# Modulation columns of the first layer: from VectorE accumulation to one-column TensorE products in three of five groups

## The chip, the cores and the metric

The kernel runs on one core of a Trainium2 chip. The metric is the device time of one execution in microseconds, the median of three runs. A profiled execution is one further run, traced by the hardware profiler. The engines are TensorE (PE, with its weight loads as PEld), VectorE (DVE), ScalarE (ACT), GpSimd (POOL) and SyncE (SP), whose queue issues the DMAs.

## The reference

The model is a trunk of two layers over 1024 tokens of width 1024, float32. At the head of each layer stands a modulated norm (adaLN), which is all that the change concerns:

```python
c_act = jax.nn.silu(c)                       # (1, 1024)
mod = c_act @ w_ada + b_ada                  # (1, 3072)
shift, scale, gate = jnp.split(mod[:, None, :], 3, axis=-1)
h = rms_norm(x, norm_g) * (1.0 + scale) + shift
proj = h @ w_in
```

The projection feeds three token mixers (pooling, retention, RWKV-7), each with a SiLU gate path; their outputs are projected, merged by sigmoid gates, projected once more, scaled by `gate` and added to x. A final RMSNorm closes the trunk.

`mod` is a product of one vector with a 1024 x 3072 matrix: very few operations on 12 MB of weights per layer.

## The kernel before

**Layout.** Features lie on the 128 partitions, tokens on the free axis. x is held as 8 tiles (kt 0 to 7, 128 features each) by 2 halves of 512 tokens. Each large product is done in three passes (high x high, low x high, high x low parts in fp32r) by `mm1` and `mm3`, and every TensorE product goes through `mmul` (line 394 of the profile).

**Modulation.** The 24 columns of `mod` (128 features each) are cut into seven groups, the list `ADA`: group 0 is scale columns 8 and 9, group 1 scale columns 10 and 11, group 2 scale columns 12 to 15, group 3 shift columns 0 to 3 (tiles kt 0 to 3), group 4 shift columns 4 to 7 (tiles kt 4 to 7), groups 5 and 6 the gate. The generator `ada` makes one group: for each kt one VectorE operation (line 216 for the first, line 218 for the other seven) multiplies a 128 x (n*128) slice of the weights by one column of the activated c and adds it to an accumulator `ada_acc`; then n TensorE products against a column of ones sum over the partitions into `adaps`, and VectorE adds the bias (line 226), and for scale columns also forms `acoef` (line 231). Each `next` on the generator does one kt, the last one the end.

**The head of layer 0, written out by hand.** From `with tc.manual_schedule` on, TensorE, VectorE, ScalarE and GpSimd work in the order in which the code stands. The norm is postponed: the first three projection tiles (low-rank, k and r of head pair 0) are computed from x scaled by `acoef` alone (`scaled`, lines 1146 and 1147; `mms(h, kt)`, blocks of nine products of 512 columns for one tile kt of half h). Meanwhile the squares of x are summed (`sq`, line 1124 on GpSimd); `rstd_task` sums them over the partitions on TensorE (`ssps`, four one-column products), takes the root on ScalarE (line 538) and the reciprocal on VectorE (line 539), and spreads the result over the partitions by four TensorE products (`rbc`). `rstd_copy` copies it to `rbs` (ScalarE, line 1157). `first_raw` multiplies the three projections by it (line 1167), and `normed` multiplies x by it (line 1176): half 0 wholly on GpSimd, half 1 four tiles on VectorE and four on GpSimd. `shifted(h, kt)` applies scale and shift and splits the result in high and low parts (lines 1184 to 1189); it needs the shift columns, group 3 for kt 0 to 3 and group 4 for kt 4 to 7. With these parts the next two projection tiles are made (`mm1` for the first of them, tile by tile for half 0). `shift_bias` makes the part of the first three projections that comes from the shift (lines 1205 and 1207).

The steps of groups 0 to 4 (`gs[0]` to `gs[4]`) are set between these. SyncE's queue loads their weights in the same order: groups 0 to 2 and two tiles of group 3 through a ring of eight slots (`ringG`), six tiles of group 3 into buffers that later hold weights (`wada`), group 4 again through the ring, then the six raw weight tiles for `shift_bias`. A ring load waits until the slot's last user has read it.

**Behind the head.** A planner orders the projection tiles and the mixers' tasks, from modelled costs and due times; a tile scheduler places the instructions. Groups 5 and 6 and all groups of layer 1 are made by `ada` on VectorE as before, in a lane of their own.

Of the kernel before, what the change touches and what calls it, by code (L numbers as in the profile page):

```python
# [17 lines left out]
P = 128  # L18
# [4 lines left out]
HF = 512  # L23
NKT = D // P
# [56 lines left out]
ADA = []  # L81
# [8 lines left out]
def trunk_kernel(ctx, tc, xT, cvec, pos, vecs, consts, w_ada, w_all, pool_w, lora_w, out):  # L90
# [16 lines left out]
    def nm(s):  # L107
        uid[0] += 1
        return f"{s}_{uid[0]}"

    def slot(tag, n, w=HF):
        def f(s, dt=F32):
            return tp.tile([P, w], dt, tag=tag, name=nm(s), bufs=n)

        return f

    t_rk = slot("rk", 4)
    t_lt = slot("lt", 4)
# [3 lines left out]
    t_vp = slot("vp", 2)  # L122
# [4 lines left out]
    def mx(s):  # L127
        t = ps_m.tile([P, HF], F32, tag="mx", name=nm(s))
        if len(mxq) == 2:
            behind[t.name] = mxq.popleft()  # L130
        mxq.append(t.name)
        return t
# [10 lines left out]
    cact = cp.tile([P, 8], F32, name="cact")  # L143
    nc.sync.dma_start(out=cact, in_=cvec)
    o = CST["bone"]
# [52 lines left out]
    def ada_load(l, g, slot_, ws, n):  # L198
        for _ in range(n):
            w = slot_("wada")  # L200
            nc.sync.dma_start(out=w, in_=w_ada[l, ADA[g][2] + len(ws)])
            ws.append(w)

    def ada(l, g, slot_, gap=2200, acc_=t_lt, ws=None):
        c, n, _ = ADA[g]
        W_ = n * P
        acc = acc_("ada_acc")[:, 0:W_]
        late = ws is None
        ws = [] if late else ws
        for kt in range(NKT):  # L210
            i, o = divmod(kt * W_, HF)
            if late and o == 0:
                ada_load(l, g, slot_, ws, min(i + 2, 2 * n) - len(ws))
            w = ws[i][:, o : o + W_]
            if kt == 0:
                nc.vector.tensor_scalar_mul(acc, w, cact[:, 0:1])
            else:
                nc.vector.scalar_tensor_tensor(acc, w, cact[:, kt : kt + 1], acc, op0=ALU.mult, op1=ALU.add)  # L218
            yield gap
        if late:  # L220
            yield wait(acc)
        ps = mx("adaps")
        for m in range(n):
            mmul(ps[:, m : m + 1], acc[:, m * P : (m + 1) * P], ones)
        o = VEC["b_ada"]
        nc.vector.tensor_tensor(mod[l][:, c : c + n], ps[:, 0:n], vec[l][:, o + c : o + c + n], op=ALU.add)
        if c >= 16:
            nc.vector.tensor_scalar_mul(mod[l][:, c : c + n], mod[l][:, c : c + n], 0.5)
        if 8 <= c < 16:
            o = VEC["norm_g"] + c - 8  # L230
            nc.vector.scalar_tensor_tensor(
                acoef[l][:, c - 8 : c - 8 + n], mod[l][:, c : c + n], 1.0, vec[l][:, o : o + n],
                op0=ALU.add, op1=ALU.mult,
            )
        yield

    def run(gen):
        for _ in gen:
            pass
# [117 lines left out]
    def wait(*aps):  # L357
        settle()
        names = [x.tensor.name if hasattr(x, "tensor") else x.name for x in aps]
        if len(mxq) == 2:  # L360
            names.append(mxq[0])
        return max(0.0, max(ready.get(n, 0.0) for n in names) - clock[0])
# [24 lines left out]
    def mmul(out, lhsT, rhs, start=True, stop=True, **kw):  # L387
        n = rhs.free_size()
        fast = rhs.dtype == F32R
        settle()  # L390
        await_(out, lhsT, rhs)
        m = lhsT.free_size()
        clock[0] += (n + 32) / 2.4 if fast else 2 * max(n, 1.6 * m - 92, m - 16) * 0.875
        nc.tensor.matmul(out, lhsT=lhsT, rhs=rhs, start=start, stop=stop, **kw)  # L394
# [113 lines left out]
    def acc_ps():  # L508
        return ps_a.tile([P, HF], F32, tag="acc", name=nm("acc"))
# [579 lines left out]
    def evac(*a):  # L1089
        run(evac_steps(*a))  # L1090
# [59 lines left out]
    def mms(h, *kts):  # L1150
        for kt in kts:
            for i in range(3):
                mm1(acc6[h][i], wparts[i][kt // 4], kt % 4, h_cur[h][kt], kt == 0, kt == 7)
# [74 lines left out]
    with tc.manual_schedule(engines={ET.PE, ET.DVE, ET.Activation, ET.Pool}):  # L1228
        acc6.append([acc_ps() for _ in range(3)])
        acc6.append([ps_c.tile([P, HF], F32, tag=t, name=nm("acc"), bufs=n) for t, n in (("cy", 2), ("cy", 2), ("ch", 1))])  # L1230
        aw = [[] for _ in range(5)]
        gs = [ada(0, g, None, acc_=t_vp if g == 4 else t_lt, ws=aw[g]) for g in range(5)]

        def aload(g, n):
            ada_load(0, g, wada_slot, aw[g], n)

        aload(0, 4)
        nc.sync.dma_start(out=vec[0], in_=vecs[0])
        wdma(0, 0)
        wsp(0, 0)  # L1240
        xdma(0, 0, 1)
        wdma(0, 1, 2)
        xdma(1, 0, 1)
        aload(1, 4)
        xdma(0, 2, 3)
        xdma(1, 2, 3)
        steps(gs[0], 9)
        derive(0)
        scaled(0, 0)
        wsp(0, 1)  # L1250
        steps(gs[1], 3)
        scaled(0, 1)
        wsp(0, 2)
        steps(gs[1], 5)
        mms(0, 0, 1)
        sq(0, 0)
        sq(0, 1)
        steps(gs[1], 1)
        scaled(1, 0, 1)
        sq(1, 0)  # L1260
        sq(1, 1)
        mms(1, 0, 1)
        aload(2, 8)
        for h in range(2):
            for kt in (2, 3):
                steps(gs[2], 2)
                scaled(h, kt)
                sq(h, kt)
        mms(0, 2, 3)
        wdma(1, 0, 1, 2)  # L1270
        xdma(0, 4, 5, 6, 7)
        nc.sync.dma_start(out=cst, in_=consts[:, 0 : CST["bone"]])
        xdma(1, 4, 5, 6, 7)
        wsp(1, 0, 1, 2)
        mms(1, 2)
        steps(gs[2], 1)
        mms(1, 3)
        for tag in ("wh", "wl"):
            for _ in range(3):
                w = wp.tile([P, HF], F32, tag=tag, name=nm("wada"), bufs=3)  # L1280
                ada_load(0, 3, lambda _: w, aw[3], 1)
        aload(3, 2)
        for kt in range(4, 8):
            sq(0, kt)
            scaled(0, kt)
            mms(0, kt)
        for kt in range(4, 8):
            sq(1, kt)
            scaled(1, kt)
            steps(gs[3], 2)  # L1290
        wprep(True)
        aload(4, 8)
        r0 = rstd_task([ssum[0]], rbc[0])
        r1 = rstd_task([ssum[1]], rbc[1])
        mms(1, 4)
        next(r0)
        mms(1, 5)
        run(r0)
        rstd_copy(0)
        steps(gs[3], 1)  # L1300
        steps(gs[4], 2)
        for i in range(3):
            first_raw(0, i)
            steps(gs[4], 1)
        normed(nc.gpsimd, 0, 0, 1, 2, 3, 4, 5, 6, 7)
        mms(1, 6)
        next(r1)
        steps(gs[4], 1)
        shifted(0, 0)
        steps(gs[4], 1)  # L1310
        shifted(0, 1)
        steps(gs[4], 1)
        mms(1, 7)
        run(r1)
        shifted(0, 2, 3)
        rstd_copy(1)
        sb = shift_bias()
        next(sb)
        first = [wready.popleft()]
        wprep()  # L1320
        first.append(wready.popleft())
        pss = {}
        for i in range(2):
            pss[i, 0] = acc_ps()
        for kt in range(4):
            mm1(pss[0, 0], first[0][1][kt // 4], kt % 4, h_cur[0][kt], kt == 0, kt == 7)
        steps(gs[4], 1)
        for kt in range(4, 8):
            shifted(0, kt)
            mm1(pss[0, 0], first[0][1][kt // 4], kt % 4, h_cur[0][kt], kt == 0, kt == 7)  # L1330
        normed(nc.vector, 1, 0, 1, 2, 3)
        normed(nc.gpsimd, 1, 4, 5, 6, 7)
        for j in range(2):
            mm3(pss[1, 0], first[1][1][j], h_cur[0][4 * j : 4 * j + 4], j == 0, j == 1)
        pss[0, 1] = acc_ps()
        for kt in range(8):
            shifted(1, kt)
            mm1(pss[0, 1], first[0][1][kt // 4], kt % 4, h_cur[1][kt], kt == 0, kt == 7)
        L_ = (0, {}, {}, [])
        evac(first[0][0], pss[0, 0], 0)  # L1340
        pss[1, 1] = acc_ps()
        for j in range(2):
            mm3(pss[1, 1], first[1][1][j], h_cur[1][4 * j : 4 * j + 4], j == 0, j == 1)
# [17 lines left out]
    for l in range(L):  # L1361
# [26 lines left out]
        while wready[0][0] != ("merge",):  # L1388
            it, ws = wready.popleft()
# [65 lines left out]
        while wready[0][0][0] != "out":  # L1455
            it, ws = wready.popleft()
# [5 lines left out]
            elif it[0] == "gate":  # L1462
                n, d = it[1], it[2]
                for h, ps in enumerate(in_tile2(ws)):
                    nc.scalar.activation(gate_tile((n, d, h)), ps, AF.Tanh, scale=0.5)
            else:
                n, d0 = it[1], it[2]
# [5 lines left out]
                for d, h in dh:  # L1473
                    ps = acc_ps()
                    mm3(ps, ws[d - d0], [osplit[n][k][h] for k in range(4)], True, True)
                    o = (d % 2) * T + h * HF
                    m = mt[d // 2][:, o : o + HF]
# [26 lines left out]
        for part, (h, sl) in enumerate(parts):  # L1504
# [3 lines left out]
            for i, d in enumerate(out_order(l, part)):  # L1508
                it, ws = wready.popleft()
# [15 lines left out]
                ps = acc_ps()[:, 0 : xr.free_size()]  # L1525
# [129 lines left out]
```

## Time and profile before

| | us |
|---|---|
| median of 3 runs (lowest, highest) | 2536.18 (2535.82, 2540.87) |
| profiled execution | 2538.03 |
| its span | 2536.3 |
| PE busy, share of the span | 2417.6, 95% |
| DVE busy | 1394.0, 55% |
| ACT busy | 796.6, 31% |
| POOL busy | 847.6, 33% |
| mean granted TensorE clock | 0.971 |

How to read it: the busy time of TensorE includes time at a lower clock. The granted clock is 1.00 at full speed and 0.50 when the throttle halves it. In the timeline a row gives start, duration, engine, line, operation, output and inputs, shape, count, and in brackets how long the engine was idle before and what ended that. Rows that follow each other on TensorE overlap, because products are pipelined: the price of one is the distance from start to start.

### The profile page before, as it was taken

Reading aid. Unit: us, or ns where it says so; the run is one execution under the profiler, and the core shown is the slowest. Engines: PE = TensorE matmul, PEld = TensorE weight load, DVE = VectorE, ACT = ScalarE, POOL = GpSimd, SP = SyncE. Lnnn points to the kernel's source line nnn. Section 1 sums busy time; section 2 is a strip of 40 time slices with the busy share of each in tenths; the row PEclk is TensorE's granted clock in tenths of the full one; section 3 lists DMA queues with packets and bytes.
Section 4 is the critical chain, followed back from the end, with each engine's and each line's share of the span. In section 5 each row is a group of like instructions: output and inputs, shape, how many; then the busy total and the mean of one; then the engine's idle time right before and its main releaser. Section 6 shows DMA issues by size and latency. Waiting matters only on the chain. (4 is left out here: it accounts for less than half of the span.)

```text
span 2536.3 us, 34936 instructions
## 1 busy us (share of the span) xinstructions
PE 2417.6 (95%) x13318; PEld 1995.5 (79%) x13318; DVE 1394.0 (55%) x2588; ACT 796.6 (31%) x1482; POOL 847.6 (33%) x729
## 2 busy tenths in 40 slices
PE   6889999999899999999999999999999999999998
PEld 4677887787788788877878787788878778787888
DVE  7886358357547935267455735844744663412344
ACT  4642232233224222212353223223322322221243
POOL 5522223133133332364452222322313322236441
PEclk9799999999999999999999999999999989999999
DMA  6222112011112413666541211211211121354342
GB/s 229 76 88 71 38 38 84 28 40 64 55 35 83 133 47 130 189 212 195 170 126 34 80 34 38 68 41 35 86 45 38 60 79 51 117 158 122 105 152 76
DMA packets 125080, 225.25 MB, mean 89 GB/s; under 512 B 14192, under 2 KB 17520, under 8 KB 124912
## 3 DMA queue, kind: packets, MB, share of 16 engines
q1 hardware_dynamic: 124912, 223.01, 27.8%
q8 instruction: 105, 1.72, 0.3%
q14 instruction: 63, 0.52, 0.1%
HBM read 176.03 MB, written 46.92 MB: 88 GB/s over the span
## 5 line engine op out<-in xcount | busy, mean ns | idle before, releaser
L513 POOL TENSOR_TENSOR wl<-wr,wh 128x512 fp32r<-128x512 f32 x338 | 450.3, 1333 | 1220.2 <-ACT wh L512 1123.0
L394 PE MATMUL acc<-hhi,wh 128*128 128x512 f32 x1968 | 799.5, 406 | 29.1 <-DVE k L981 29.1
L394 PE MATMUL acc<-hlo,wh 128*128 128x512 f32 x1968 | 801.7, 407 | 0.0
L394 PE MATMUL acc<-hhi,wl 128*128 128x512 f32 x1968 | 799.2, 406 | 0.0
L394 PEld LDWEIGHTS acc<-hhi,wh 128*128 128x128 f32 x1968 | 377.7, 192 | 100.4 <-DVE k L981 31.6
L512 ACT CAST wh<-wr 128x512 fp32r<-128x512 f32 x338 | 209.3, 619 | 734.3 <-PE acc L394 476.0
L394 PEld LDWEIGHTS acc<-hhi,wl 128*128 128x128 f32 x1968 | 377.6, 192 | 68.8 <-issue 2.2
L394 PEld LDWEIGHTS acc<-hlo,wh 128*128 128x128 f32 x1968 | 377.2, 192 | 68.8 <-issue 1.3
L394 PE MATMUL acc<-olo,wh 128*128 128x512 f32 x384 | 154.2, 402 | 5.8 <-POOL olo L513 5.8
L394 PE MATMUL acc<-oG,wh 128*128 128x512 f32 x384 | 153.1, 400 | 3.5 <-ACT oG L512 1.7
L394 PE MATMUL acc<-oG,wl 128*128 128x512 f32 x384 | 152.5, 398 | 0.0
L936 DVE SCALAR_TENSOR_TENSOR S<-ch,pc,SP 64x64 f32<-64x64 f32 x256 | 72.5, 283 | 105.0 <-PE ch L394 98.5
L925 DVE TENSOR_TENSOR xst<-cy,MT 64x128 f32<-64x128 f32 x128 | 36.1, 282 | 168.7 <-PE cy L394 168.4
L922 ACT ACTIVATE SP<-S,pc 128x128 f32<-128x128 f32 x128 | 51.4, 402 | 179.1 <-DVE S L936 175.1
L858 DVE TENSOR_TENSOR tm<-MT 64x30 f32<-64x30 f32 (+14 forms) x240 | 100.2, 417 | 7.6
L864 DVE TENSOR_TENSOR MT<-MT,tm 64x30 f32<-64x30 f32 (+14 forms) x240 | 95.2, 397 | 7.8
L931 DVE COPY Z<-ch 64x128 f32<-64x128 f32 x128 | 36.1, 282 | 112.3 <-PE ch L394 111.7
L394 PEld LDWEIGHTS acc<-olo,wh 128*128 128x128 f32 x384 | 73.2, 191 | 24.6 <-POOL olo L513 8.9
L394 PEld LDWEIGHTS acc<-oG,wh 128*128 128x128 f32 x384 | 73.2, 191 | 22.7 <-ACT oG L512 2.9
L1482 DVE SCALAR_TENSOR_TENSOR gs<-gs,acc 128x512 f32<-128x512 f32 x64 | 43.5, 682 | 85.8 <-PE acc L394 74.6
L218 DVE SCALAR_TENSOR_TENSOR ada_acc<-wada,cact,ada_acc 128x512 f32<-128x512 f32 (+1 forms) x68 | 70.0, 1029 | 31.9 <-DMA wada<-in_w_ada 31.0
L394 PEld LDWEIGHTS acc<-oG,wl 128*128 128x128 f32 x384 | 73.6, 192 | 16.6
(292 smaller groups left out, 3825.3 us busy)
## 6 DMA issues: line engine op xcount, KB each, us to landing
wr<-in_w_all SPq DMA_DIRECT2D x364, 256.0 KB, 2.7
gd<-gsg SPq DMA_DIRECT2D x80, 256.0 KB, 2.0
gs<-gd SPq DMA_DIRECT2D x80, 256.0 KB, 2.9
wada<-in_w_ada SPq DMA_DIRECT2D x70, 256.0 KB, 3.0
ol<-od SPq DMA_DIRECT2D x64, 256.0 KB, 2.9
ringG<-in_w_ada SPq DMA_DIRECT2D x26, 256.0 KB, 5.3
x<-in_xT SPq DMA_DIRECT2D x16, 256.0 KB, 5.4
od<-po SPq DMA_DIRECT2D x16, 256.0 KB, 2.1
```

What stands on the lines that cost most here:

```text
L218: nc.vector.scalar_tensor_tensor(acc, w, cact[:, kt : kt + 1], acc, op0=ALU.mult, op1=ALU.add)
L394: nc.tensor.matmul(out, lhsT=lhsT, rhs=rhs, start=start, stop=stop, **kw)
L512: nc.scalar.copy(hi, src)
L513: eng.tensor_tensor(lo, src, hi.bitcast(F32), op=ALU.subtract)
L858: nc.vector.tensor_tensor(pr, M3[:, i + 1 :, i : i + 1].to_broadcast([64, n, i]), M3[:, i : i + 1, 0:i].to_broadcast([64, n, i]), op=ALU.mult,
L864: nc.vector.tensor_tensor(M3[:, i + 1 :, 0:i], M3[:, i + 1 :, 0:i], pr, op=ALU.add)
L922: nc.scalar.activation(SP, S, AF.Copy, scale=pcc)
L925: nc.vector.tensor_tensor(xst[0:64, :], cy[0:64, 0:P], AV[:, c * P : (c + 1) * P], op=ALU.add)
L931: nc.vector.tensor_copy(Z[0:64, c, :], ch[0:64, 0:P])
L936: nc.vector.scalar_tensor_tensor(Sn[rw, rw], ch[rw, P + 64 * hd : P + 64 * hd + 64], pc[rw, c : c + 1], SP[rw, rw], op0=ALU.mult, op1=ALU.add,
L1482: nc.vector.scalar_tensor_tensor(s, s, 1.0, ps, op0=ALU.add, op1=ALU.mult)
```

## The change

Groups 0, 3 and 4 of layer 0 are made by a new generator, `ada_pe`. For each kt it issues n TensorE products at once: the 128 x 128 weight slice is the stationary operand, the column of the activated c the moving one, and all eight kt accumulate in `adaps`. There is no accumulator tile and no product against ones. The end (bias, `acoef`) is moved to `ada_end`, which both generators call. Groups 1 and 2 stay with `ada`. And `mms(1, 6)`, the block of nine products for tile 6 of half 1, is moved: it stood behind half 0's broadcast and the GpSimd products, and now stands ahead of the broadcast.

```diff
+    def ada_pe(l, g, ws):
+        c, n, _ = ADA[g]
+        W_ = n * P
+        ps = mx("adaps")
+        for kt in range(NKT):
+            i, o = divmod(kt * W_, HF)
+            for m in range(n):
+                mmul(
+                    ps[:, m : m + 1], ws[i][:, o + m * P : o + (m + 1) * P], cact[:, kt : kt + 1],
+                    start=(kt == 0 and m == 0), stop=(kt == NKT - 1 and m == n - 1), skip_group_check=True,
+                )
+            yield
+        ada_end(l, c, n, ps)
+        yield
...
-        gs = [ada(0, g, None, acc_=t_vp if g == 4 else t_lt, ws=aw[g]) for g in range(5)]
+        gs = [(ada(0, g, None, ws=aw[g]) if g in (1, 2) else ada_pe(0, g, aw[g])) for g in range(5)]
...
         mms(1, 4)
         next(r0)
         mms(1, 5)
+        mms(1, 6)
         run(r0)
         rstd_copy(0)
         steps(gs[3], 1)
...
         normed(nc.gpsimd, 0, 0, 1, 2, 3, 4, 5, 6, 7)
-        mms(1, 6)
         next(r1)
```

In the changed program's order TensorE has 16 products of group 0 at its very start; 32 of group 3 behind half 0's block of tile 7 and ahead of half 1's block of tile 4; 20 of group 4 behind half 0's broadcast, then half 1's sums of squares, then the other 12 and half 1's block of tile 7.

More of the change, by code (lines that the diff above doesn't have):

```diff
@@ L224, in ada, with ada_end @@
             mmul(ps[:, m : m + 1], acc[:, m * P : (m + 1) * P], ones)
+        ada_end(l, c, n, ps)
[12 more added lines that the diff above has]
+            yield
+        ada_end(l, c, n, ps)
+        yield
+    def ada_end(l, c, n, ps):
         o = VEC["b_ada"]
@@ L234, in ada @@
             )
-        yield
     def run(gen):
```

## The prediction

> **What bounds the kernel now.** I read the page's chain of waits first, then the busy time by stretch, then the timeline of each engine from 0 to 130 us.
>
> ```profile
> PE 13%; DVE 0%; POOL 0%; issue 0%; ACT 0%; DVEq 0%; ACTq 0%; POOLq 0%
> ```
>
> ```profile
> 0.00:43.00 43.00, 25.15 (x85) 18.58 (x86) 31.09 (x48) 17.15 (x29) 20.28 (x20) 0.92 0.94 334
> 43.00:107.00 64.00, 49.19 (x188) 39.30 (x188) 59.76 (x79) 32.73 (x55) 39.37 (x29) 0.76 0.19 61
> 64.00:74.00 10.00, 10.00 (x36) 8.74 (x36) 7.26 (x9) 2.30 (x5) 8.13 (x6) 0.50 0.42 141
> 108.00:120.00 12.00, 12.00 (x55) 9.84 (x54) 9.22 (x23) 8.46 (x15) 4.26 (x5) 1.00 0.19 54
> 2080.00:2100.00 20.00, 20.00 (x146) 15.16 (x145) 0.00 (x0) 4.06 (x7) 0.00 (x0) 0.50 0.04 14
> ```
>
> The chain that ends last is TensorE work. The stretches (columns: PE, PEld, DVE, ACT, POOL busy, granted clock, DMA share, GB/s) show three stages. Up to 43 us the DMA engines are 94% busy. From 43 to 107 VectorE is busy 59.76 of 64 us and TensorE runs at a mean clock of 0.76. From about 99 us on TensorE runs without gaps (12.00 of 12 at clock 1.00). What the change is worth is how much earlier or later that dense stream gets going; I find nothing behind it that would absorb a shift.
>
> **The change part by part.** *Removed.* The same view for the accumulators' tile alone:
>
> ```profile
> 43.00:107.00 64.00, 3.41 (x16) 3.78 (x16) 19.65 (x16) 0.76 0.19 61
> ```
>
> Groups 3 and 4 are 16 VectorE operations of 19.65 us in the stage that VectorE fills. That is the most that could be won. What it would unlock:
>
> ```profile
> 62.85 0.17 DVE L539 RECIPROCAL rn<-rn 128x4 f32<-128x4 f32 x1
> ...
> 77.87 0.58 ACT L1157 COPY rbs<-rbc 128x512 f32<-128x512 f32 x1
> 78.35 1.14 ACT L512 CAST wh<-wr 128x512 fp32r<-128x512 f32 x2
> ...
> 89.34 0.81 ACT L1187 ACTIVATE x<-x,mod,acoef 128x512 f32<-128x512 f32 x1 [8.14 <-DVE mod L226]
> ```
>
> ScalarE stood 8.14 us for group 4's columns, and half 0's norm factor left VectorE only at 62.85, behind group 3's chain.
>
> *Added.* A group of 4 columns becomes 8 x 4 = 32 products, and each fp32 product is two passes (a group's 4 products are x8 below): 64 passes for group 3, 64 for group 4, 32 for group 0. The price of a pass:
>
> ```profile
> 40.65 1.07 PE L394 MATMUL adaps<-fixed,ada_acc 128*128 128x1 f32 x8
> 41.58 0.48 PE L394 MATMUL acc<-hhi,wbig 128*128 128x512 f32 x1
> ...
> 53.92 0.95 PE L394 MATMUL ssps<-fixed,sq 128*128 128x1 f32 x8
> 54.73 0.48 PE L394 MATMUL acc<-hhi,wbig 128*128 128x512 f32 x1
> ...
> 63.12 2.05 PE L394 MATMUL rbc<-cst,rn 128*128 128x128 f32 x8 [5.65 <-issue]
> 64.96 1.71 PE L394 MATMUL adaps<-fixed,ada_acc 128*128 128x1 f32 x8
> 66.53 0.77 PE L394 MATMUL acc<-hhi,wbig 128*128 128x512 f32 x1
> ...
> 67.53 1.05 PE L394 MATMUL acc<-hhi,wbig 128*128 128x512 f32 x2
> 68.38 0.63 PE L394 MATMUL acc<-hlo,wbig 128*128 128x512 f32 x1
> ...
> 70.51 1.70 PE L394 MATMUL ssps<-fixed,sq 128*128 128x1 f32 x8
> 72.07 0.77 PE L394 MATMUL acc<-hhi,wbig 128*128 128x512 f32 x1
> ```
>
> Start to next start over 8: (41.58 - 40.65)/8 = 0.116 and (54.73 - 53.92)/8 = 0.101 us at full clock, I take 0.11; (66.53 - 64.96)/8 = 0.196 and (72.07 - 70.51)/8 = 0.195 at half clock. A 512-column product is (68.38 - 67.53)/2 = 0.43 at half clock; at full clock the six blocks of nine from 41.58 to 53.92 take 2.06 each (0.23 per product), against 3.84 at half. So a group's stream costs 64 x 0.11 = 7.0 or 64 x 0.196 = 12.5 us, where VectorE paid about 10.
>
> *Which clock.* From 64 to 74 TensorE is busy without a gap, yet that row grants it 0.50 throughout: blocks of 512-column products broken by one-column passes did not open the clock. The row 2080:2100 is 20 us of wide products between streams of small ones, again at 0.50, and just before it the clock is seen to fall:
>
> ```profile
> 2074.87 0.39 PE L394 MATMUL acc<-hhi,wl 128*128 128x512 f32 x1
> 2075.19 1.19 PE L394 MATMUL m<-MT,G 32*32 32x32 f32 x32
> ...
> 2077.20 1.19 PE L394 MATMUL m<-MT,G 32*32 32x32 f32 x32
> ...
> 2078.33 0.54 PE L394 MATMUL acc<-hhi,wh 128*128 128x512 f32 x1
> 2078.66 0.63 PE L394 MATMUL acc<-hlo,wh 128*128 128x512 f32 x1
> ```
>
> Products grow from 0.39 to 0.63 us within 3.5 us of the first small ones, with no idle time. Nothing in this trace is as bare as 64 one-column passes on end; between the ends 7.0 and 12.5 per stream I take the behaviour nearest to these rows: the clock halves after 3 us (2 to 6) of stream, and wide products on end reopen it after some 4 to 5 (in 108:120 it is 1.00).
>
> The Trainium skill, "TensorE: Matmul & The Clock Gate" (section "Why this matters for your kernels"), says to keep TensorE busy for 4 us or more to be past the gate; the added streams are just that, so by its words they would open the clock; the rows 64:74 and 2080:2100 disagree, and the rule is the first rival below. The same page, § LDWEIGHTS, gives 128 columns / 1.2 = 107 ns per weight load whatever the clock; the full-clock rows agree (0.10 to 0.12), the half-clock rows do not (0.196); by the page, as an estimate, a stream would be 6.8 us in either state.
>
> *The path, times in the span of before.* Group 0: 32 passes at half clock, 6.3 us, starting when its first tile and the activated vector are there.
>
> ```profile
> 3.99 0.17 DVE L195 TENSOR_TENSOR cact<-cact,cth 128x8 f32<-128x8 f32 x1
> ...
> 10.12 0.16 DVE L226 TENSOR_TENSOR mod<-adaps,vec 128x2 f32<-128x2 f32 x1 [1.10 <-PE adaps L394]
> ...
> 13.44 1.37 DVE L216 TENSOR_SCALAR ada_acc<-ringG,cact 128x256 f32<-128x256 f32 x1 [1.17 <-DMA ringG<-in_w_ada]
> ```
>
> 4.2 + 6.3 + 0.3 gives the add at 10.8 instead of 10.12. I cost it at nothing: VectorE's next chain waits for a DMA until 13.44. Without that cover it is 0.7 us.
>
> Group 3's stream now stands in TensorE's order ahead of half 1's block of tile 4. Five blocks from 41.58 end at 51.9; 3 us at 0.11 are 27 passes, the other 37 take 7.3: 62.2. Queued behind it: block 4 (3.84, 66.0), the sums of squares of half 0 (1.57, 67.6), block 5 (3.84, 71.4), the moved block 6 (2.06 with the clock back, 73.5; 3.84 without). Only then come half 0's eight broadcast passes. VectorE's reciprocal is early now, so it is no longer what they wait for.
>
> ```profile
> 65.20 0.58 ACT L1157 COPY rbs<-rbc 128x512 f32<-128x512 f32 x1 [10.04 <-PE rbc L394]
> ...
> 65.87 12.36 POOL L1176 TENSOR_TENSOR x<-x,rbs 128x512 f32<-128x512 f32 x8 [7.71 <-ACT rbs L1157]
> ...
> 79.05 3.21 POOL L513 TENSOR_TENSOR wl<-wr,wh 128x512 fp32r<-128x512 f32 x2
> 82.23 6.34 POOL L1176 TENSOR_TENSOR x<-x,rbs 128x512 f32<-128x512 f32 x4
> ```
>
> From their start at 63.12 to the end of the copy at 65.78 was 2.66 us at half clock, about 1.5 at full: 75.0 to 76, that is **9 to 10 us later**. GpSimd's eight products start there.
>
> Then group 4: 40 passes, 4.4 us while the clock lasts, from 74.5 to 78.9; half 1's sums 1.57, 80.4; 24 passes at 0.196, 85.1; block 7, 3.84, 89.0; broadcast and copy, 90.7. Against 78.45 half 1's norm factor is **12 us later**. Group 4's columns are ready at about 85, so the 8.14 us wait is gone, but ScalarE reaches tile 4 only behind that copy and two casts (1.14): 91.9 instead of 89.34, 2.5 us late. What was saved on VectorE is spent in TensorE's queue.
>
> GpSimd's order behind the copy is two subtractions and four products, 3.21 + 6.34: they ran from 79.05 to 88.57, and now run from about 92 to 101.5, beside VectorE operations that had VectorE to themselves:
>
> ```profile
> 91.26 1.76 DVE L1189 TENSOR_TENSOR hlo<-x,hhi 128x512 fp32r<-128x512 f32 x1
> ...
> 95.86 0.68 DVE L1189 TENSOR_TENSOR hlo<-x,hhi 128x512 fp32r<-128x512 f32 x1
> ...
> 96.46 2.48 DVE L1176 TENSOR_TENSOR x<-x,rbs 128x512 f32<-128x512 f32 x4
> ...
> 98.80 0.46 PE L394 MATMUL acc<-hhi,wh 128*128 128x512 f32 x1
> ```
>
> The same subtraction is 1.76 beside GpSimd and 0.68 alone. The changed order has ten VectorE operations from tile 4's subtraction (about 93 now) to tile 7's; at 0.9 us each they end near 102 instead of 96.5. Half 1's products and shifts follow them, so the dense stream, which began at 98.80, comes **5 to 9 us late; I take 8**. Behind it the two programs' orders differ by a few exchanged products up to some 190 us, for which I take +1 (-1 to +3). The ring's loads wait for TensorE's reading instead of VectorE's and land some 8 us later, but their users are later too.
>
> Sum: 0 + 8 + 1 = **+9 us**. The profiled execution took 2538.03 (span 2536.3), 1.85 above the median of the runs shown, so it would become 2547 and the median **2545**.
>
> **The rivals.** (1) *The streams hold the clock.* Group 3 ends at 51.9 + 7.0 = 58.9; blocks and sums at full clock (2.06 + 0.8 + 4.1) 65.8; copy at 67.3, only 1.5 late; group 4's passes end near 74.5, half 1's copy at 78.3, as before. Group 4's add stands behind four subtractions on VectorE, the last of which ended at 86.2 with accumulations among them:
>
> ```profile
> 82.74 3.42 DVE L1189 TENSOR_TENSOR hlo<-x,hhi 128x512 fp32r<-128x512 f32 x2
> ...
> 89.10 0.15 DVE L226 TENSOR_TENSOR mod<-adaps,vec 128x4 f32<-128x4 f32 x1
> ```
>
> Without those it comes at about 85 instead of 89.1. So -4 there, +1 of order: 2533, within 0.2%. For it: one-column passes at 53.92 ran at full clock, but only eight. Against: the two half-clock rows. This is also the time of the page's 4 us rule.
> (2) *The opposite side: the freed VectorE decides.* If the clock holds and ScalarE's wait of 8.14 goes whole, the dense stream starts 8 us sooner: 2528. It decides if group 4's add comes at 81 or earlier, which needs GpSimd's eight products done by 76; they have taken 12.36 from a start no earlier than 65.9, though 7.26 of 10 us of VectorE's work ran beside them, so it is possible but tight.
> (3) *The clock never reopens before 102.* Block 6 costs 1.8 more, the first 24 dense products (24 x 0.2) 4.8 more: about +15, 2551.
>
> **How the numbers follow.** Forecast 0.58, rival 1 0.22, rival 2 0.11, rival 3 0.09. The range takes in the forecast with its 5 to 9 and -1 to +3, rivals 1 and 3: 2532 to 2554. A measurement of this kernel tells about 0.2% (5 us) from no change. Faster 0.12 (rival 2 and an edge of 1), same 0.24 (the rest of 1 and the forecast's low end), slower 0.64.
>
> **What would show it.** In the changed profile: a granted clock of 0.50 from about 56 to 70 us, over a busy TensorE; group 3's passes ending near 62 (59 refutes the clock step); half 0's copy at 75, half 1's at 91; an idle VectorE between 56 and 75; no wait of ScalarE for group 4's columns; GpSimd's last four products at 95 to 101. If the copies are at 67 and 78, rival 1 holds and the forecast is wrong; if the dense stream starts before 93, rival 2.

## The result and the profile after

The changed kernel takes **2546.31 us** (median of 9 runs, 2540.05 to 2554.52) against 2535.82 of the kernel before (9 runs beside it): ratio 1.0046, 95% interval 1.0027 to 1.0064. It is 10.5 us slower. In the experiments below, one of the 12 runs of e4_g4 (3920 us) and one of e10_latefix (10311 us) lie far outside all others and are left out of the ratios. The profiled execution of the changed kernel is a low one, 2540.05 (span 2538.2). Far behind the head it was spared a stretch at half clock:

```profile
2080.00:2100.00 20.00, 20.00 (x226) 15.74 (x224) 1.39 (x1) 5.69 (x10) 2.56 (x2) 1.00 0.18 64
```

The same 20 us ran at 0.50 in the profile of before. So the spans of single executions are not compared below. Instead I use three landmarks of each profile (copies of the norm factor, start of the dense stream, first `av` products at 255 us) and the medians.

The busy time by stretch of the changed kernel (columns PE, PEld, DVE, ACT, POOL, granted clock, DMA share, GB/s):

```profile
43.00:107.00 64.00, 57.85 (x268) 50.36 (x267) 34.33 (x49) 24.06 (x40) 34.77 (x28) 0.71 0.21 62
54.00:58.00 4.00, 4.00 (x38) 3.96 (x36) 2.42 (x2) 0.00 (x0) 3.92 (x4) 1.00 0.00 0
60.00:72.00 12.00, 12.00 (x41) 10.45 (x42) 0.22 (x2) 0.27 (x1) 0.00 (x0) 0.50 0.27 89
74.00:78.00 4.00, 4.00 (x35) 3.85 (x34) 1.49 (x3) 0.59 (x1) 1.51 (x2) 1.00 0.09 21
80.00:92.00 12.00, 12.00 (x49) 11.13 (x49) 8.10 (x20) 5.59 (x9) 6.83 (x7) 0.50 0.37 111
100.00:110.00 10.00, 6.16 (x14) 4.18 (x15) 10.00 (x14) 2.81 (x5) 4.89 (x7) 0.50 0.15 52
```

VectorE went from 59.76 busy us of 64 to 34.33; from 60 to 72 it, ScalarE and GpSimd do almost nothing. TensorE went from 49.19 to 57.85 and its mean clock from 0.76 to 0.71: it is busy 12.00 of 12 us in both rows that the clock halves. From 100 to 110 all is turned round: TensorE has gaps, and VectorE is full beside GpSimd. TensorE's timeline shows the streams:

```profile
54.11 5.79 PE L412 MATMUL adaps<-cact,wada 128*128 128x1 f32 x48
59.76 3.55 PE L412 MATMUL adaps<-cact,ringG 128*128 128x1 f32 x16
63.17 0.77 PE L412 MATMUL acc<-hhi,wbig 128*128 128x512 f32 x1
...
75.62 5.03 PE L412 MATMUL adaps<-cact,ringG 128*128 128x1 f32 x40
80.51 1.84 PE L412 MATMUL ssps<-fixed,sq 128*128 128x1 f32 x8
82.22 5.26 PE L412 MATMUL adaps<-cact,ringG 128*128 128x1 f32 x24
87.34 0.77 PE L412 MATMUL acc<-hhi,wbig 128*128 128x512 f32 x1
...
107.83 0.63 PE L412 MATMUL acc<-hhi,wh 128*128 128x512 f32 x1
...
109.54 0.63 PE L412 MATMUL acc<-hlo,wh 128*128 128x512 f32 x1
109.97 0.49 PE L412 MATMUL acc<-hhi,wl 128*128 128x512 f32 x1
110.30 0.40 PE L412 MATMUL acc<-hhi,wh 128*128 128x512 f32 x1
```

The price of a pass at full clock is read where the clock is 1.00 throughout. The same view for the tile `adaps` alone:

```profile
54.00:59.00 5.00, 4.89 (x45) 4.96 (x45) 0.00 (x0) 1.00 0.00 0
```

That is 4.89/45 = 0.11 us. After the clock has fallen, a pass costs (63.17 - 59.76)/16 = 0.213 or (87.34 - 82.22)/24 = 0.213 from start to next start. The 40 passes from 75.62 to 80.51, 0.122 on average, have the fall among them (rows 74:78 and 80:92). Group 3's stream takes 9.06 us, and the dense stream starts at 107.83, 9.0 us late; its first products still run at half clock, 0.43 us from start to start. Between them stand the two copies on ScalarE, GpSimd's work that hangs on them, and VectorE's:

```profile
75.82 0.59 ACT L1175 COPY rbs<-rbc 128x512 f32<-128x512 f32 x1 [6.66 <-PE rbc L412]
...
93.27 0.59 ACT L1175 COPY rbs<-rbc 128x512 f32<-128x512 f32 x1 [5.16 <-PE rbc L412]
...
94.80 0.82 ACT L1205 ACTIVATE x<-x,mod,acoef 128x512 f32<-128x512 f32 x1
```

```profile
76.48 10.29 POOL L1194 TENSOR_TENSOR x<-x,rbs 128x512 f32<-128x512 f32 x8 [17.72 <-ACT rbs L1175]
...
94.46 2.52 POOL L531 TENSOR_TENSOR wl<-wr,wh 128x512 fp32r<-128x512 f32 x2 [7.63 <-ACT wh L530]
96.94 6.08 POOL L1194 TENSOR_TENSOR x<-x,rbs 128x512 f32<-128x512 f32 x4
```

```profile
11.22 0.16 DVE L245 TENSOR_TENSOR mod<-adaps,vec 128x2 f32<-128x2 f32 x1 [7.08 <-PE adaps L412]
...
13.04 1.38 DVE L216 TENSOR_SCALAR ada_acc<-ringG,cact 128x256 f32<-128x256 f32 x1
...
76.51 1.89 DVE L1185 TENSOR_TENSOR raw<-acc,rbs 128x512 f32<-128x512 f32 x3 [7.09 <-ACT rbs L1175]
...
90.80 2.71 DVE L1225 SCALAR_TENSOR_TENSOR bacc<-ringG,mod,bacc 128x128 f32<-128x128 f32 x10
96.67 0.85 DVE L1207 TENSOR_TENSOR hlo<-x,hhi 128x512 fp32r<-128x512 f32 x1 [3.17 <-ACT hhi L1206]
97.45 1.50 DVE L1203 TENSOR_SCALAR x<-x,acoef,mod 128x512 f32<-128x512 f32 x1
...
103.69 1.75 DVE L1207 TENSOR_TENSOR hlo<-x,hhi 128x512 fp32r<-128x512 f32 x1
...
106.69 2.48 DVE L1194 TENSOR_TENSOR x<-x,rbs 128x512 f32<-128x512 f32 x4
```

Half 0's copy ends at 76.41 (before 65.78), half 1's at 93.86 (78.45). GpSimd's last two subtractions and four products run from 94.46 to 103.0, and the ten VectorE operations from 96.67 to 106.69 take 10.0 us beside them. Behind the head the shift goes on unabsorbed, as the first `av` products show, in the kernel before and in the changed one:

```profile
255.42 1.14 PE L394 MATMUL av<-Z,G 64*64 64x64 f32 x16
```

```profile
267.30 1.14 PE L412 MATMUL av<-Z,G 64*64 64x64 f32 x16
```

That is 11.9 us late in these two profiles; the medians differ by 10.5 us.

### The profile page after: what moved, and what is told of

Its sections match the earlier page's. It is cut to its first block, busy times and chain, and to the rows that moved or that the text cites. A ratio compares the mean times of both kernels' runs of the same rounds, so it can differ in the third digit from the quotient of the medians.

```text
span 2538.2 us, 35181 instructions
## 1 busy us (share of the span) xinstructions
PE 2429.5 (96%) x13458; PEld 2011.0 (79%) x13458; DVE 1371.8 (54%) x2564; ACT 797.2 (31%) x1482; POOL 844.3 (33%) x729
## 5 line engine op out<-in xcount | busy, mean ns | idle before, releaser
L412 PEld LDWEIGHTS ch<-xst,G 128*128 128x128 f32 x512 | 76.9, 191 | 11.3 <-DVE xst L943 0.2
```

## The experiments

**The theory** is the prediction's: the one-column streams let the clock halve; so the norm factors come late; so GpSimd's work falls beside VectorE's subtractions, and these start the dense stream late. **Rivals**: the streams' place in TensorE's queue is the cost, at any clock; the moved block is the cost; only one of the groups is. All the times in one table (copy ends, starts of the dense stream and of the `av` products from each kernel's profile; medians of 12 runs, of 9 for the changed kernel; beside each four kernels 35 runs of the kernel before, with medians of 2535.3 to 2535.8; the ratio is estimated from the two sets of runs and is not the quotient of the two medians):

| kernel | copy 0 | copy 1 | dense | av | median | ratio (interval) |
|---|---|---|---|---|---|---|
| before | 65.78 | 78.45 | 98.80 | 255.42 | 2535.8 | |
| changed | 76.41 | 93.86 | 107.83 | 267.30 | 2546.31 | 1.0046 (1.0027 to 1.0064) |
| e6_wide | 71.94 | 82.94 | 102.44 | 255.29 | 2533.76 | 0.9991 (0.9975 to 1.0008) |
| e7_late | 59.74 | 75.57 | 94.36 | 251.81 | 2538.34 | 1.0014 (0.9996 to 1.0032) |
| e8_latewide | 61.07 | 72.05 | 92.64 | 252.61 | 2538.33 | 1.0011 (0.9993 to 1.0029) |
| e1_move | 63.60 | 73.91 | 95.06 | 250.70 | 2532.14 | 0.9992 (0.9975 to 1.0008) |
| e2_streams | 74.33 | 93.85 | 108.23 | 262.85 | 2546.48 | 1.0053 (1.0031 to 1.0075) |
| e3_g3 | 71.45 | 79.93 | 101.93 | 261.86 | 2542.90 | 1.0026 (1.0006 to 1.0046) |
| e4_g4 | 66.47 | 93.24 | 107.60 | 260.18 | 2536.03 | 1.0003 (0.9984 to 1.0022) |
| e15_dve1 | 77.12 | 94.58 | 103.94 | 260.48 | 2536.57 | 1.0012 (0.9988 to 1.0037) |
| e9_widedve | 68.01 | 79.02 | 95.01 | 255.40 | 2537.07 | 1.0013 (0.9994 to 1.0032) |
| e10_latefix | 61.10 | 72.08 | 92.93 | 252.99 | 2539.31 | 1.0008 (0.9992 to 1.0024) |
| e13_dve_bias | 68.04 | 79.05 | 91.76 | 252.12 | 2537.22 | 1.0014 (0.9994 to 1.0034) |
| e14_late_bias | 63.28 | 74.26 | 91.09 | 248.04 | 2529.90 | 0.9981 (0.9958 to 1.0004) |

The intervals are some 8 to 12 us wide; a difference of 3 us between two medians decides nothing.

The landmarks are of one execution each, and they scatter too. Ahead of the streams TensorE has a stretch at half clock, which ends at different times. The row from 41 to 48 us in the kernel before, the changed one, e6_wide and e9_widedve:

```profile
41.00:48.00 7.00, 7.00 (x35) 5.92 (x35) 5.04 (x6) 5.85 (x11) 4.30 (x3) 1.00 0.32 114
41.00:48.00 7.00, 7.00 (x28) 5.91 (x27) 4.20 (x6) 5.01 (x9) 3.47 (x3) 0.69 0.37 132
41.00:48.00 7.00, 7.00 (x21) 5.79 (x21) 2.99 (x5) 3.80 (x7) 2.34 (x2) 0.50 0.27 96
41.00:48.00 7.00, 7.00 (x36) 5.90 (x35) 4.87 (x6) 5.69 (x10) 4.14 (x3) 1.00 0.27 93
```

The last two kernels have the same order up to half 0's copy, yet that copy ends at 71.94 in one and at 68.01 in the other. So a landmark can move by some 4 us with no change in the kernel.

### The clock: the same passes, 128 columns wide (e6_wide)

The changed kernel, with each pass's moving column repeated 128 times; of each block of 128 equal result columns the first is read back.

```diff
-    ps[:, m : m + 1], ws[i][...], cact[:, kt : kt + 1],
+    ps[:, m * P : (m + 1) * P], ws[i][...], cact[:, kt : kt + 1].to_broadcast([P, P]),
...
-        ada_end(l, c, n, ps)
+        ada_end(l, c, n, ps[:, 0 : n * P : P])
```

> The changed kernel with one thing different: the moving operand of the three groups' products is the activated column repeated 128 times instead of once, so each pass streams 128 columns (the bias is added from the first column of each). Same order, same number of passes. If the clock is what the one-column streams cost: the granted clock stays at 1.00 through group 3's and group 4's passes, group 3 takes about 7 us instead of 9.1, half 0's copy of the norm factor comes at about 67 instead of 75.8, half 1's at about 78 instead of 93.3, the dense stream begins at 96 to 100, and the time is within 4 us of the kernel before (2532 to 2540). If only the place of the passes in TensorE's queue counts: the passes take as long or longer, the copies stay at 75 and 90 or later, and the time stays at 2543 to 2552.

Measured: the loss is gone, 2533.76. The stretches of this kernel that hold its two streams, and the first stream on TensorE's timeline:

```profile
56.00:66.00 10.00, 10.00 (x82) 9.59 (x80) 1.60 (x1) 0.00 (x0) 3.94 (x3) 1.00 0.25 73
70.00:80.00 10.00, 10.00 (x86) 9.80 (x85) 7.59 (x12) 3.92 (x7) 7.99 (x7) 1.00 0.64 184
```

```profile
56.01 5.52 PE L413 MATMUL adaps<-cact,wada 128*128 128x128 f32 x48
61.37 1.95 PE L413 MATMUL adaps<-cact,ringG 128*128 128x128 f32 x16
63.07 0.48 PE L413 MATMUL acc<-hhi,wbig 128*128 128x512 f32 x1
```

The clock stays at 1.00 through both. A pass with 128 times the columns costs (63.07 - 56.01)/64 = 0.110 us: as much as a one-column pass at full clock, and about half of one at half clock. The number of instructions, their places and their weights are the same, so the width of the moving operand decides the clock. The copies and the dense stream come later than expected (71.94, 82.94 and 102.44, the last 3.6 us behind the kernel before), but 3.9 us of this stand ahead of the streams, in the half-clock stretch shown above. e9_widedve, with the same order up to half 0's copy and the clock at 1.00 from 41 us on, has the copies at 68.01 and 79.02. Against the kernel before, the streams at full clock and the moved block together thus cost the two copies 2.2 and 0.6 us; in the changed kernel the copies are 10.6 and 15.4 us late. The greater part of the loss is the clock.

### The place: both streams behind the broadcasts (e7_late, e8_latewide)

Group 3's nine steps go behind half 0's copy, group 4's behind half 1's. In these two kernels group 3's last two weight tiles are read after their ring slots were refilled with group 4's first two, so shift columns 0 to 3 are summed from other weights; the instructions are the same.

```diff
         for kt in range(4, 8):
             sq(1, kt)
             scaled(1, kt)
-            steps(gs[3], 2)
...
         rstd_copy(0)
-        steps(gs[3], 1)
-        steps(gs[4], 2)
+        steps(gs[3], 9)
...
         run(r1)
+        rstd_copy(1)
         shifted(0, 2, 3)
-        rstd_copy(1)
+        steps(gs[4], 9)
```

The single steps of group 4 between these places are taken out; e8_latewide has the wide passes as well.

> The changed kernel with one-column products as they are, but group 3's stream moved whole behind half 0's broadcast and copy, and group 4's whole behind half 1's. If the place in the queue is the larger part: half 0's copy at about 61, half 1's at 76 to 80, the dense stream at 94 to 97, time 2 to 5 us below the kernel before (about 2532). If the clock is the larger part: it still falls to 0.50 inside both streams (about 64 to 72 and 80 to 90), the first tiles behind them run at half clock, the dense stream begins no earlier than 99 and the time is at or above the kernel before (2536 to 2544).

> Both edits: the streams behind the broadcasts, and 128 columns per pass. If clock and place are separate costs: half 0's copy at about 60, half 1's at about 70, the dense stream at 89 to 92, time 6 to 10 us below the kernel before (about 2528). If either one is the whole cost, this one is not faster than the better of the two alone.

Measured: the copies come at 59.74 and 75.57 with one-column passes, and at 61.07 and 72.05 with wide ones; both are earlier than in the kernel before, and the dense streams start 4.4 and 6.2 us before that of the kernel before. So the place is a second way out: behind the copies even a stream at half clock no longer delays the dense stream, although half 1's copy, which stands behind group 3's stream, still comes 3.5 us later than with wide passes. The times that went with this outcome (about 2532 and 2528) were missed: the medians are 2538.3, no better than before. What the head won is not in them; the last experiments take that up.

### The moved block (e1_move, e2_streams)

The kernel before with the move alone, and the changed kernel without it:

```diff
         mms(1, 5)
+        mms(1, 6)
         run(r0)
...
-        mms(1, 6)
         next(r1)
```

> The kernel before with only the block of tile 6 of half 1 moved ahead of half 0's broadcast, all groups on VectorE. By the prediction's working the block falls into the 5.65 us in which TensorE waited for the reciprocal, so half 0's copy stays at 65 to 66 and half 1's at 76 to 79; time within 3 us of the kernel before. If the move is part of the loss, the copy of half 0 comes 2 to 4 us later and the time rises by as much.

> The changed kernel without the move: block 6 of half 1 stands again behind half 0's broadcast. My working: half 0's copy 2 us earlier than in the changed kernel (about 74), half 1's copy and everything behind it where they are (93, dense stream at 106 to 108), time 2543 to 2548. If the move carries part of the loss: half 1's copy 3 us or more earlier, time 2542 or less.

Measured: 2532.14 for the move alone, 2546.48 for the streams without it. The copy of half 0 is 2.08 us earlier in e2_streams than in the changed kernel, that of half 1 is the same (93.85, 93.86). The move is not the loss. In e1_move the copies came earlier than expected (63.60 and 73.91 against 65 to 66 and 76 to 79); 3.3 us under the kernel before by the medians is inside the interval, so whether the move alone is a small gain stays open.

### One group at a time (e3_g3, e4_g4)

The kernel before with group 3 alone, or group 4 alone, made by `ada_pe`:

```diff
-        gs = [ada(0, g, None, acc_=t_vp if g == 4 else t_lt, ws=aw[g]) for g in range(5)]
+        gs = [(ada_pe(0, g, aw[g]) if g == 3 else ada(0, g, None, acc_=..., ws=aw[g])) for g in range(5)]
```

> Group 3 alone as one-column products, nothing else changed (block 6 back behind half 0's broadcast). My path (the end of half 1's copy and GpSimd's last four products decide): the stream halves the clock some 5 us after its start, half 0's copy is 7 to 9 us late (73 to 75), half 1's copy only 2 to 4 late (80 to 82), the dense stream 0 to 4 late, time 2535 to 2540. If what counts is that the first stream pushes everything behind it in TensorE's queue: the dense stream 8 to 10 late as in the changed kernel, time 2544 to 2548. If the one-column products only pay off where VectorE is relieved and the clock is no matter: faster than before, 2528 to 2532.

> Group 4 alone as one-column products, nothing else changed. My path: half 0's copy where it was before (65 to 66), half 1's copy 9 to 11 us late (87 to 90) since the stream stands ahead of half 1's sums and block 7 and runs at 0.196 us a pass; GpSimd's last four products move beside VectorE's subtractions, the dense stream 5 to 9 us late, time 2541 to 2546: most of the whole change's loss. If the first stream carries the loss: the dense stream within 2 us of before, time 2533 to 2538.

In the head the dense streams came about as my path said: 3.1 us late with group 3 alone (first copy 5.7 late instead of 7 to 9, second 1.5 instead of 2 to 4), 8.8 with group 4 alone (second copy 14.8 late, more than the 9 to 11 expected, since the clock was still at half when the stream began). The times did not: 2542.90, not 2535 to 2540, and 2536.03, not 2541 to 2546. Between the dense stream and the `av` products e3_g3 loses another 3.3 us and e4_g4 gets 4.0 back. The waits of TensorE between 99 and 230 us (in all, times, longest) show where the two differ, in e3_g3:

```profile
PE g L412 <- ACT BKt L837: 4.6, 1, 4.6
```

and in e4_g4, where it is another product, `pps`, that waits for that copy:

```profile
PE pps L412 <- ACT BKt L837: 1.7, 1, 1.7
```

In the kernel before, that wait of `g` is 1.7 us, in the changed one 3.3. Which products stand behind the copy `BKt` is a matter of the order that the planner's part of the program comes out with, and it differs from kernel to kernel. The two kernels lack the move, so their sum is to be held against e2_streams: by the `av` landmark 6.4 + 4.8 = 11.2 against 7.4, by the medians 7.6 + 0.7 = 8.3 against 10.7. With the scatter of both measures this does not say how the loss divides. What is shown: group 4's stream alone delays the dense stream by more than a landmark's scatter, but not the median (interval 0.9984 to 1.0022); with group 3 alone the 3.1 us are within that scatter, but the median is slower (1.0006 to 1.0046). So the dense stream's start alone does not give the time.

### GpSimd beside VectorE (e15_dve1)

The changed kernel, one-column passes and all, with half 1's four GpSimd products on VectorE:

```diff
-        normed(nc.gpsimd, 1, 4, 5, 6, 7)
+        normed(nc.vector, 1, 4, 5, 6, 7)
```

> The changed kernel (one-column products) with half 1's four GpSimd norm products on VectorE, behind the other four. If the term of GpSimd beside VectorE is right: VectorE's ten operations from tile 4's subtraction to tile 7's, 9.4 us in the changed kernel, take 5 to 6; the dense stream starts at 103 to 104 instead of 107.8; the four added products (2.5 us) come behind that and are partly hidden; time 2541 to 2544. If those operations were slow for another reason: dense stream at 107 or later, time 2546 to 2549.

Measured: 2536.57; most of the loss is gone, though the streams and copies are where they were (77.12, 94.58) and the clock is 0.50 from 60 to 72 as in the changed kernel. VectorE's timeline of this kernel:

```profile
97.39 0.85 DVE L1207 TENSOR_TENSOR hlo<-x,hhi 128x512 fp32r<-128x512 f32 x1 [3.16 <-ACT hhi L1206]
98.16 0.54 DVE L1203 TENSOR_SCALAR x<-x,acoef,mod 128x512 f32<-128x512 f32 x1
98.62 0.34 DVE L1225 SCALAR_TENSOR_TENSOR bacc<-ringG,mod,bacc 128x128 f32<-128x128 f32 x1
...
102.64 0.68 DVE L1207 TENSOR_TENSOR hlo<-x,hhi 128x512 fp32r<-128x512 f32 x1
103.24 4.90 DVE L1194 TENSOR_TENSOR x<-x,rbs 128x512 f32<-128x512 f32 x8
```

The ten operations take 5.85 us (97.39 to 103.24) instead of 10.0; the dense stream starts at 103.94, 3.9 us earlier, and the `av` products 6.8 earlier. The last link of the theory holds; the further 2.9 us arise behind the dense stream's start, where the order of the products is another one, and were not traced. The median gives back 9.7 us, but its interval (0.9988 to 1.0037) is wide enough for 7.

### What the head can gain (e9_widedve, e10_latefix, e13_dve_bias, e14_late_bias)

Two repairs with wide passes. e9_widedve: the changed kernel's order, half 0's eight norm products on VectorE. e10_latefix: the order of e8_latewide with group 4's last two loads behind group 3's stream.

```diff
-        normed(nc.gpsimd, 0, 0, 1, 2, 3, 4, 5, 6, 7)
+        normed(nc.vector, 0, 0, 1, 2, 3, 4, 5, 6, 7)
```

```diff
-        aload(4, 8)
+        aload(4, 6)
...
         steps(gs[3], 9)
+        aload(4, 2)
```

> The changed kernel with the moving column repeated 128 times (clock held) and half 0's eight norm products on VectorE, which stands idle there, instead of GpSimd. If VectorE operations beside GpSimd are what keeps the wide version from a gain (the same operations 1.3 to 1.75 us beside it, 0.34 to 0.68 alone): the products take about 5 us instead of 10 on VectorE, group 4's add comes at about 85 instead of 92.5, the dense stream 5 to 8 us before the wide version's, time 2527 to 2531. If the order of TensorE's queue alone sets the head: as the wide version, 2532 to 2536.

> Wide products, with group 3's stream behind half 0's broadcast and group 4's behind half 1's copy (group 4's last two loads behind group 3's stream). Both copies early (60 to 62 and 71 to 74) at a clock of 1.00, the dense stream 4 to 7 us before the kernel before. If the head's gain is carried to the end as its loss is: 2529 to 2532. If a later wait takes part of it (at about 187 us TensorE waits for a transposed copy of ScalarE whose chain starts from VectorE's work in the head): 2533 to 2538.

Measured: dense streams at 95.01 and 92.93, and no gain, 2537.07 and 2539.31, above what was expected in either case. (Of the 7.4 us by which e9_widedve's dense stream leads that of e6_wide, 3.9 are the stretch ahead of the streams.) In both, VectorE's order is the new bound: operations of the shift's bias, which nobody needs yet, stand ahead of what TensorE waits for. VectorE in e9_widedve:

```profile
79.06 0.15 DVE L246 TENSOR_TENSOR mod<-adaps,vec 128x4 f32<-128x4 f32 x1
79.14 9.87 DVE L1226 SCALAR_TENSOR_TENSOR bacc<-ringG,mod,bacc 128x128 f32<-128x128 f32 x10
88.93 0.68 DVE L1208 TENSOR_TENSOR hlo<-x,hhi 128x512 fp32r<-128x512 f32 x1
```

and in e10_latefix, where they stand ahead of the add of group 4's columns:

```profile
81.89 2.96 DVE L1226 SCALAR_TENSOR_TENSOR bacc<-ringG,mod,bacc 128x128 f32<-128x128 f32 x3
84.77 0.15 DVE L246 TENSOR_TENSOR mod<-adaps,vec 128x4 f32<-128x4 f32 x1
```

In e9_widedve group 4's columns are there at 79.1, but tile 4's subtraction comes at 88.93. Ten such operations took 2.71 us in the changed kernel (at 90.80), where GpSimd stood still. So, in both kernels, the bias operations are held behind half 1's shifts:

```diff
     def shift_bias():
...
+        yield
         ps = mx("bias")
...
         for kt in range(8):
             shifted(1, kt)
             mm1(...)
+        next(sb)
```

> Wide products, half 0's norm products on VectorE, and the 24 VectorE operations of the shift's bias held back behind half 1's subtractions. In the run without the last step ten of them (9.9 us beside GpSimd) stood between group 4's columns and tile 5's subtraction. If VectorE's order is now the bound of the head: the dense stream at 87 to 89 instead of 94, time 2529 to 2533. If the later wait at about 190 us takes it: the gain is gone by 200 us, time 2535 to 2538.

> Wide products placed behind the broadcasts, and the bias operations held back in the same way. Group 4's columns come at 79 instead of 84.8, the dense stream at 86 to 88 (98.8 in the kernel before), time 2527 to 2532 if the head's gain is carried on; 2535 to 2539 if the later wait takes it, since the held-back bias also holds back the first mixer's inputs.

Measured: e13_dve_bias 2537.22 (dense stream 91.76, later than the 87 to 89 expected: its subtractions now run beside GpSimd's products), e14_late_bias **2529.90**, 5.9 us under the kernel before (0.9981, 0.9958 to 1.0004) and some 16 under the changed one. Group 4's columns are added at 80.81 (79 expected). Its dense stream starts 7.7 us early, also later than expected (86 to 88), its `av` products 7.4 early:

```profile
58.00:82.00 24.00, 24.00 (x184) 22.73 (x183) 8.23 (x16) 9.73 (x17) 15.74 (x14) 1.00 0.42 118
```

```profile
248.04 1.14 PE L413 MATMUL av<-Z,G 64*64 64x64 f32 x16
```

It is the fastest version run, though its interval just reaches 1. In e10_latefix and e13_dve_bias, of 5.9 and 7.0 us at the dense stream 2.4 and 3.3 are left at the `av` products, and none in the medians. That the medians of e7_late, e8_latewide and e10_latefix lie 2.9 to 4.0 us over before while their `av` products come 2.4 to 3.6 early was not settled; half-clock stretches far behind the head, such as the one at 2080 us, differ from profile to profile (0.50 in that of before, 1.00 in the changed kernel's) and are as large.

## Why the prediction was right

The time was forecast at 2545 and is 2546.31; the mechanism was the forecast one, and the signs it named are in the profile, up to 3 us off. That the time was met so closely is in part luck, since misses of 1 to 2 us cancel and the median's interval is some 9 us wide. By its steps:

- **Price of a pass.** 0.11 us at full clock, measured 0.11; at half clock 0.196, measured 0.213, slightly more.
- **The clock.** It was to halve 3 us (2 to 6) into a stream. The row 54:58 has 1.00, 60:72 has 0.50; by the row 54:59 it held for the first 4.9 us of group 3's stream (in e2_streams for 2.6, in e7_late for 5.3), and by 74 it had reopened, behind wide products, as forecast. e6_wide and e9_widedve show that this is the greater part of the cost, and the place in the queue the smaller. The Trainium skill, "TensorE: Matmul & The Clock Gate" (section "Why this matters for your kernels"), has it that 4 us of continuous work get TensorE past the gate; the traces agree for passes of 128 columns, as far as the clock stayed open (1.00 through 56:66 and 70:80), and not for one-column passes (0.50 through 60:72 and 80:92, busy 12.00 of 12).
- **Group 0 at nothing.** Its add came at 11.22 instead of 10.8. VectorE's next chain did not wait for it: it began at 13.04. But ScalarE's first scaled tile did, and came at 11.61 instead of 10.76, which the forecast did not look at; whether these 0.85 us reach the end is not shown.
- **Half 0's copy** at 75 to 76: 76.41. This is two misses that cancel. Group 3's stream began 2.2 us later than worked out (54.1, not 51.9), since the half-clock stretch ahead of it lasted longer than in the profile of before (0.69 in 41:48 against 1.00); and it took 9.1 instead of 10.3, since the clock fell later. How much of the delay hangs on that start is open: in e2_streams the stream starts at 52.45, and the dense stream is no earlier (108.23).
- **Half 1's copy** at 90.7: 93.86. This is the largest miss inside the chain. Group 4's passes began 1.1 us late, the clock fell within the first 40 of them (4.9 us instead of 4.4), the other 24 took 5.1 instead of 4.7, and the broadcast and copy, at half clock, 2.5 instead of 1.7.
- **GpSimd beside VectorE.** Forecast 92 to 101.5, measured 94.46 to 103.0; ten operations at 0.9 us, measured 1.0. e15_dve1 shows what this link carries: without it, the half-clock streams cost 5.1 us at the dense stream instead of 9.0, and 5.1 instead of 11.9 at the `av` products.
- **Dense stream** 8 us late (5 to 9): 9.0.
- **Order behind it** +1 (-1 to +3): by the `av` products it is 11.9 - 9.0 = +2.9. In it are a longer wait for `BKt` (3.3 us against 1.7) and the first products of the dense stream at half clock, about 1.1 us up to 110.30, which the forecast had left out.

The sum was 9 and the medians say 10.5; both terms came out at the upper end of their bounds. Rival 1, that the streams hold the clock, was priced at 2533, and e6_wide, in which they do, takes 2533.76. That agreement is luck in part: the rival had the dense stream 4 us early, and in e6_wide it is 3.6 late. Rivals 2 and 3 fall by the profile of the changed kernel: the dense stream starts at 107.83 and not before 93, and the clock is 1.00 in 74:78. One sentence was too strong: "I find nothing behind it that would absorb a shift". For a delay it held. Gains were partly absorbed, by waits some 90 us later (in e10_latefix `g` waits 4.6 us for `BKt`); of 19.65 us of VectorE work removed, the best version here keeps 5.9 by the medians, with an interval that reaches 1.

## What to carry to other kernels

Work moved to an engine with gaps is paid at the price of that engine's queue and clock: ask what stands behind it in the queue, and whether its shape holds the clock. Where a stream of one-column products must stand ahead of something that others wait for, widen it for the clock's sake, or put it behind; here either one removed the loss, and neither alone made a gain that the medians show. And look for what a late release pushes side by side: here ten VectorE operations took 10.0 us beside GpSimd's work and 5.85 without most of it.

## What the runs showed of the hardware

A one-column pass and a 128-column pass took the same time at full clock (0.11 us both), so the wider operand was free. At half clock a one-column pass took 0.213. TensorE, busy without a gap, was granted 0.50 with one-column passes (12.00 of 12 us) and 1.00 with 128 columns (10.00 of 10).

The slowing of VectorE beside GpSimd seems to depend on where the operands lie; no run varied this alone. The subtraction `hlo` from two tiles in SBUF took 1.75 us beside GpSimd's products and 0.68 alone. But the three `raw` products at 76.51 in the changed kernel, which read their first operand from the accumulators, took 1.89 together, 0.63 each, although GpSimd's eight products had started at 76.48. Two inputs in SBUF are not the only case: the `TENSOR_SCALAR` of line 1203, with one tile as input, took 1.50 us at 97.45 beside GpSimd's products and 0.54 in e15_dve1 at 98.16. The Trainium skill, "SBUF — State Buffer" (section "Who interferes with whom"), tells of one pair of ports that VectorE and GpSimd hold by turns; in the section "SBUF: two separate sides" VectorE needs it, among others, for operations with two SBUF inputs, and the rows of `hlo` and `raw` agree.
